# Norm scales spread by transposes of whole tiles, and a convolution whose seven-product jobs keep the program's order on TensorE

## The chip, the cores and the metric

The kernel runs on one core of a Trainium2 chip. The metric is the device time of one execution in microseconds (us); less is better. Before the change the median of three runs is 1405.58 us (1405.56 to 1406.27). The profile comes from one more execution, which took 1405.36 us.

## The reference

The program is one inference step of a decoder with two layers. It works on 512 new prompt tokens and on 8 short sequences of 4 tokens each (32 sample tokens), with the same weights, 1024 channels and all numbers in float32. The first layer mixes by a short gated convolution, the second by retention, and each is followed by a gated feed-forward block. Cut to what matters here:

```
def rmsnorm(x, g):
    y = x * rsqrt(mean(x * x, axis=-1) + 1e-6)
    return y * g

def short_conv_mixer(x, buf, w_in, w_conv, w_out):
    b, c, h = split(x @ w_in, 3)
    full = concatenate([buf, c * h], axis=1)
    y = sum(w_conv[j] * full[:, j:j + L] for j in range(3))
    return (b * y) @ w_out

x = x + mixer(rmsnorm(x));  x = x + swiglu(rmsnorm(x))      # per layer
return rmsnorm(x), states
```

The outputs are the normalised activations and the new states of the convolution and of the retention.

## The kernel before, in words

**Layout.** Activations are kept transposed: eight tiles `x[0..7]` of 128 channels by 544 tokens (512 prompt tokens and 32 sample tokens), each treated as two halves of 272 columns (`HT`). A float32 product is made out of three TensorE products of a faster format: each operand is split into a high and a low part (`split`, L201 to L204: ScalarE rounds, VectorE subtracts), and high by high, high by low and low by high are added in PSUM. Weights come from memory by loads on SyncE's queue and are split in the same way. In `mixed` (L312 to L318) one half of a weight's low part comes from VectorE, and the other from ScalarE (a negated copy) and an adding transfer that GpSimd issues.

**The norm.** `rms_scale` sums the squares of each token over the channels by products with a column (L272), takes the power -0.5 on GpSimd, and has then one scale per token, with 128 tokens down the partitions in one column of `rN`. The scales are needed along the free axis, the same in all 128 partitions. `spread` (L250 to L254) does this with a float32 TensorE product: the column, repeated 128 times, is the stationary operand, and columns `lo:hi` of an identity are streamed. Six spreads cover 544 tokens, because the third tile of tokens lies across the two halves; some are 16, 32 and 112 columns wide. ScalarE copies the result to `R` (L284). `rms_scale` runs four times (convolution, first feed-forward block, retention, second feed-forward block). The final norm calls `spread` in its own function `scale`, three times for each half (L933 to L935).

**Seven-product jobs.** Most of the big matrix products are made by a scheme that multiplies two-by-two blocks with seven block products instead of eight. A `Job` (L364 to L420) makes 256 output channels out of 1024 input channels. It has weights for seven products, which `prepare` makes (`weights7`, L320 to L360: two loads, four VectorE sums, four splits). Each product is 4 channel blocks by 3 parts, so 12 matmuls of 272 columns (`product`, L380 to L393). The results accumulate in three PSUM tiles: `a` takes products 1, 6, 7 and 4 one after the other, `c` takes 5 and 3, and `b` takes 2. After most of them ScalarE or VectorE has to read the tile (`take`, in `summed`, L437 to L450) before the next product adds to it: the first three reads are ScalarE copies (L445), the later ones VectorE additions (L447). `begin` makes product 1, `middle` makes 6, 5, 2 (in an order that can be set; 2, 5, 6 in the convolution's first job) and 7, and `end` makes 3 and 4.

**The order of the work.** `run` (L422 to L435) interleaves the jobs: prepare the next job's weights, the middle of this job, the beginning of the next, the end of this one. In the program's order TensorE's products of two neighbouring jobs n and n+1 are therefore: n's 6, 5, 2, 7; 1 of n+1; n's 3, 4; 6, 5, 2, 7 of n+1; and so on. That isn't yet the order on the chip. The library in which the kernel is written plans each engine's queue while the program is built: among the instructions that it holds to be ready it takes those that stand earlier in the program, and where the earlier ones wait by its reckoning it lets later ones pass. Once planned, a queue's order is fixed. `with tc.issue_after(i):` sets a bound to this planning: what is traced inside the block is queued behind instruction `i` on `i`'s engine. It adds no wait on the chip.

**The convolution.** The first pair of channel tiles, and one third of the second pair, are made by plain products (`project`, L187). Then come eight jobs (L644): two for the rest of the second pair and three for each of the other two pairs. The third job of a pair ends with gating (`mixed_in`, L576 to L582), the second with the convolution's taps (`taps`, L557 to L574), which is a chain of ScalarE and VectorE work. Here the jobs are numbered J0 to J7, and J1:4 is the product 4 of J1. In the trace the product can be told by its operands: `sm<-parts,wh` is 1 or 2, `mm<-parts,h` is 3, `sm<-oh,wh` is 7 or 4, `sm<-oh,h` is 6 and `mm<-oh,h` is 5 (with `ol` or `wl`, `l` in the second and third part). (`oh`, `ol` and `parts` are activations; `wh`, `wl`, `h` and `l` are weights.) The output projection and its loads follow, and then the feed-forward block, whose jobs are of the same class.

Of the kernel before, what the change touches and what calls it, by code (L numbers as in the profile page):

```python
# [12 lines left out]
P = 128  # L13
D = 1024
KT = D // P
SEQ = 512
NB = 8
DS = 4
NS = NB * DS
# [4 lines left out]
HT = T // 2  # L24
# [28 lines left out]
def hybrid_decode_kernel(ctx: ExitStack, tc: tile.TileContext, a: dict, o: dict):  # L53
    nc = tc.nc
# [12 lines left out]
    kinds, at = ["m"], [0]  # L67

    def wide(kind):

        kinds[0], at[0] = kind, 0

    def psum():

        kind = kinds[0][at[0] % len(kinds[0])]
        at[0] += 1
        if kind == "s":
            return [bank(), bank()]
# [21 lines left out]
    mask_s, ident, mean_w = rest[:, :NS], rest[:, NS : NS + P], rest[:, NS + P :]  # L100
# [33 lines left out]
    rN = resid.tile([P, 6], F32, tag="rN", name="rN")  # L134
# [112 lines left out]
            nc.vector.tensor_add(out, var, eps)  # L247
        nc.gpsimd.tensor_tensor(out, out, expo[: out.shape[0], :n], op=ALU.pow)

    def spread(out, tt, lo, hi):  # L250

        return nc.tensor.matmul(
            out, rN[:, tt : tt + 1].to_broadcast([P, P]), ident[:, lo:hi], start=True, stop=True, skip_group_check=True
        )  # L254

    def rms_scale(sample=False, pt=None, rest=4):

        n = 6 if sample else 5  # L260
        pt = pt or psum()
        ms = half(pt, 0)[:, 496:502]
        cols = [slice(tt * P, (tt + 1) * P) for tt in range(4)] + [slice(T - P, T), slice(SEQ, T)]
        for tt in range(n):
            lhs = sqacc[:, cols[tt]]
            if tt == 5:
                lhs = sqlast[:, :P]
                nc.vector.tensor_copy(
                    lhs.rearrange("p (g c) -> p g c", c=NS),
                    sqacc[:, SEQ:].unsqueeze(1).to_broadcast([P, P // NS, NS]),  # L270
                )
            nc.tensor.matmul(ms[:, tt : tt + 1], lhs, mean_w[:, 0:1], start=True, stop=True)  # L272
            if tt < n - 1:
                yield
        rsqrt(rN[:, :n], ms[:, :n], n)
        for _ in range(rest):
            yield

        for tt, hf, at, lo, hi in (
            (0, 0, 0, 0, P), (1, 0, P, 0, P), (2, 0, 2 * P, 0, HT - 2 * P),  # L280
            (2, 1, 0, HT - 2 * P, P), (3, 1, 3 * P - HT, 0, P), (4, 1, SEQ - HT, P - NS, P),
        ):
            spread(half(pt, hf)[:, at : at + hi - lo], tt, lo, hi)
        each(lambda p, r: nc.scalar.activation(r, p, AF.Copy), pt, R)  # L284

    def drain(steps):
# [77 lines left out]
    class Job:  # L364
# [8 lines left out]

        order = (6, 5, 2)
        weave = iter(())

        def prepare(self, adding=False):
            self.w = weights7(*self.srcs, self.sw, len(self.ks) * P, adding, **self.places)

        def product(self, out, which, first):  # L380
            wh, wl = self.w[which]
            for j, k in enumerate(self.ks):
                c = slice(j * P, (j + 1) * P)
                bh, bl = self.operand(k, which)
                for i, (w, b) in enumerate(((wh, bh), (wh, bl), (wl, bh))):
                    last = nc.tensor.matmul(  # L386
                        out, w[:, c], b,
                        start=(first and j == 0 and i == 0), stop=(j == len(self.ks) - 1 and i == 2),
                        skip_group_check=True,
                    )  # L390
                if which not in (5, 6, 2):
                    with tc.issue_after(last.ins):
                        next(self.weave, None)  # L393
# [60 lines left out]
    with ExitStack() as c0:  # L454
# [134 lines left out]
        c, b = temp("c"), temp("b")  # L589
# [52 lines left out]
        turn = [0]  # L642
        pair[1] = c2
        jobs = [job(f, j) for f in range(2, KT, 2) for j in (1, 2, 0) if f > 2 or j != 1]  # L644
        wide("m")
        jobs[0].prepare()
        with ExitStack() as order:
# [14 lines left out]
        for i, n in enumerate(PAIRED[0]):  # L662
            if i < 2:
                wh, wl, pt = early[i]
                project(pt, wh, wl, 0, yh, yl, first=False, ks=(KT - 2, KT - 1))
            else:
                wh, wl = load_piece(a["cvout"][n], KT * P)
                pt = psum()
# [219 lines left out]
    def final(ms, acts, group_weights, fp, tp):  # L888

        ah, al = acts  # L890
        ws = [group_weights(n, ms) for n in range(KT - LATE, KT)]

        sums = {}

        def products(hf):
            c = slice(hf * HT, (hf + 1) * HT)
            for n in range(KT - LATE, KT):
                wh, wl = ws[n - KT + LATE]
                pt = [None, None]
                pt[hf] = bank()  # L900
                project(pt, wh, wl, 0, ah, al, hfs=(hf,))
                nc.vector.tensor_add(x[n][:, c], x[n][:, c], half(pt, hf)[:, :HT])
                square_sum(n, tp, "gu", 4, c=c, add=nc.vector, join=not hf)
                yield

        def gained(hf):

            c = slice(hf * HT, (hf + 1) * HT)
            y = [fp.tile([P, 4, HT], F32, tag="f", name=nm("ya")), tp.tile([P, 4, HT], F32, tag="gu", name=nm("yb"))]
            for kt in range(KT):  # L910
                with tc.issue_after(last_square[0].ins) if hf and kt == KT - 2 else ExitStack():
                    nc.scalar.activation(y[kt // 4][:, kt % 4, :], x[kt][:, c], AF.Copy, scale=g_fin(kt))
            return y

        def scale(hf):
            pt = bank()
            mq = pt[:, 496:499]

            of = (sqacc, sqlast)[: hf + 1]
            for t in of:  # L920
                for i, at in enumerate((0, P, HT - P)):
                    cols = slice(hf * HT + at, hf * HT + at + P)
                    last_sum[hf] = nc.tensor.matmul(
                        mq[:, i : i + 1], t[:, cols], mean_w[:, 0:1], start=t is of[0] and (hf == 0 or i == 0),
                        stop=t is of[-1], skip_group_check=True,
                    )
                if t is not of[-1]:
                    yield
            with tc.issue_after(first_product[0].ins) if hf else ExitStack():
                nc.vector.tensor_scalar_add(rN[:, :3], mq, EPS)  # L930
            powers[hf] = nc.gpsimd.tensor_tensor(rN[:, :3], rN[:, :3], expo[:, :3], op=ALU.pow)
            yield
            for i, (lo, hi) in enumerate(((0, P), (0, P), (3 * P - HT, P))):  # L933
                last_spread[0] = spread(pt[:, i * P : i * P + hi - lo], i, lo, hi)
            sums[hf] = pt[:, :HT]  # L935

        def copied(hf):

            with tc.issue_after(last_square[0].ins):
                nc.scalar.activation(R[:, hf, :], sums[hf], AF.Copy)  # L940

        def out(hf, y, w):

            yy = y[w // 2][:, w % 2 * 2 : w % 2 * 2 + 2, :]
            if w == 0:
                for i in range(2):
                    nc.gpsimd.tensor_tensor(yy[:, i, :], yy[:, i, :], R[:, hf, :], op=ALU.mult)
            else:
                made = nc.vector.tensor_mul(yy, yy, sums[hf].unsqueeze(1).to_broadcast([P, 2, HT]))
                first_product[0] = first_product[0] or made  # L950
# [12 lines left out]
        drain(products(0))  # L963
        first, second = scale(0), products(1)
        next(second)
        next(first)
        y0 = gained(0)
        drain(second)
        drain(first)
        out(0, y0, 1)  # L970
        with tc.issue_after(first_product[0].ins):
            copied(0)
        rest = scale(1)
        with tc.issue_after(last_spread[0].ins):
            next(rest)
        next(rest)
        idle(5, last_sum[1].ins)
        y1 = gained(1)
        out(0, y0, 2)
        out(0, y0, 3)  # L980

        with tc.issue_after(last_store[0].ins), tc.issue_after(powers[1].ins):
            out(0, y0, 0)
        drain(rest)
        copied(1)
        for w in range(4):
            out(1, y1, w)
# [782 lines left out]
```

## Time and profile before

| what | value |
|---|---|
| median of three runs | 1405.58 us (1405.56 to 1406.27) |
| the profiled execution | 1405.36 us |
| its span, first to last instruction | 1403.6 us |
| the plain products of the convolution | about 1 to 58 us |
| the convolution's eight jobs | 58 to 146 us |
| output projection, first feed-forward block | 146 to about 550 us |
| retention | about 550 to 1027 us |
| last output products, second feed-forward block, final norm | 1027 us to the end |

In the profile's rows PE is TensorE's matmuls, PEld its weight loads, DVE VectorE, ACT ScalarE, POOL GpSimd, SP SyncE; "DMA_DIRECT2D" on POOL or SP is the issue of a transfer. A row of the timeline gives the start in us, the duration in us, engine, line, operation, output and inputs, shapes, and how many instructions were merged. Idle time before a row and what ended it stand in brackets. A matmul's row is longer than the step to the next one, since matmuls overlap; the step is read from the starts.

### The profile page before, as it was taken

How to read it: one execution, taken by the hardware profiler on the slowest of the kernel's cores; microseconds unless marked ns; L12 is line 12 of the kernel's file. 1: busy time of each engine (PE TensorE's matmuls, PEld its weight loads, DVE VectorE, ACT ScalarE, POOL GpSimd, SP SyncE). 2: the span in 40 equal slices, each digit the busy share in tenths (PEclk: the TensorE clock that was granted, in tenths of full speed). 3: DMA queues.
4: the chain of work that ended last, by engine and by line, in shares of the span. 5: the costliest groups of instructions: out<-in, count | busy, mean ns of one | idle time of the engine just before them, and what ended most of it. 6: DMA issues, size and time to landing. Idle time of an engine off the chain costs nothing.

```text
span 1403.6 us, 26578 instructions
## 1 busy us (share of the span) xinstructions
PE 1390.2 (99%) x10454; PEld 1317.3 (94%) x10454; DVE 1132.1 (81%) x1923; ACT 822.9 (59%) x1286; POOL 219.4 (16%) x255
## 2 busy tenths in 40 slices
PE   9999999999999999999999999999999999999997
PEld 8999999999999999999967877877899999999997
DVE  6987889898989878676867576586799898989884
ACT  7666567667677657666632313224387767677654
POOL 0111011212221213111200000000111212121212
PEclk9999999999999999999999999999999999999999
DMA  6476346777676754677667355465766777777742
GB/s 206 119 169 166 108 106 159 168 173 183 143 188 151 168 120 134 185 199 201 212 212 240 121 209 184 144 235 181 211 143 153 169 176 172 154 184 153 165 106 87
DMA packets 99295, 233.69 MB, mean 166 GB/s; under 512 B 9793, under 2 KB 33489, under 8 KB 98785
## 3 DMA queue, kind: packets, MB, share of 16 engines
q1 hardware_dynamic: 68032, 167.47, 38.4%
q0 software_dynamic: 28688, 56.61, 23.5%
q10 hardware_dynamic: 2448, 7.91, 1.5%
q8 instruction: 82, 1.34, 0.4%
q14 instruction: 45, 0.36, 0.1%
HBM read 191.84 MB, written 28.42 MB: 157 GB/s over the span
## 4 chain that ended last, share of the span: by engine, by line
PE 93%; DVE 2%; issue 2%; DMA 2%; POOL 0%; ACT 0%; SPq 0%; DVEq 0%; POOLq 0%; ACTq 0%
PE sm L386 43%; PE mm L386 16%; PE mm L187 14%; PE sm L187 4%; PE sm L1262 2%; PE sm L1264 2%; PE sm L1263 2%; PE sm L175 2%; PE sm L177 1%; PE sm L176 1%; PE sm L1483 1%; DVE S L1506 1%; PE mm L1270 1%; DMA wl<-in_rtout_dram 1%; PE mm L1422 0%
## 5 line engine op out<-in xcount | busy, mean ns | idle before, releaser
L386 PE MATMUL sm<-oh,wh 128*128 128x272 f32 x856 | 247.8, 289 | 0.5 <-DVE b L447 0.5
L386 PE MATMUL sm<-ol,wh 128*128 128x272 f32 x856 | 246.1, 288 | 0.0
L386 PE MATMUL sm<-oh,wl 128*128 128x272 f32 x856 | 246.1, 287 | 0.0
L202 ACT ACTIVATE h<-w 128x1024 fp32r<-128x1024 f32 (+3 forms) x170 | 136.5, 804 | 106.3 <-PE mm L386 92.9
L203 DVE TENSOR_TENSOR l<-w,h 128x1024 fp32r<-128x1024 f32 (+3 forms) x170 | 153.6, 904 | 28.1 <-ACT h L202 25.3
L315 ACT ACTIVATE wh<-w 128x1024 fp32r<-128x1024 f32 (+1 forms) x134 | 133.7, 998 | 56.7 <-PE sm L386 48.5
L386 PEld LDWEIGHTS sm<-oh,wh 128*128 128x128 f32 x856 | 161.3, 188 | 2.0 <-DVE b L447 0.9
L386 PEld LDWEIGHTS sm<-oh,wl 128*128 128x128 f32 x856 | 161.1, 188 | 0.0
L386 PEld LDWEIGHTS sm<-ol,wh 128*128 128x128 f32 x856 | 160.8, 188 | 0.1
L386 PE MATMUL sm<-parts,wh 128*128 128x272 f32 x736 | 142.5, 288 | 0.0
L202 ACT ACTIVATE wh<-w 128x1024 fp32r<-128x1024 f32 (+3 forms) x76 | 68.0, 898 | 120.3 <-PE mm L187 62.1
L318 POOL DMA_DIRECT2D wl<-in_ffgu_dram x87 | 81.7, 939 | 328.2 <-ACT wl L317 94.2
L386 PE MATMUL mm<-oh,h 128*128 128x272 f32 x396 | 115.5, 292 | 0.0
L386 PEld LDWEIGHTS sm<-parts,wh 128*128 128x128 f32 x736 | 115.5, 188 | 0.0
L386 PE MATMUL mm<-oh,l 128*128 128x272 f32 x396 | 113.5, 287 | 0.0
L386 PE MATMUL mm<-ol,h 128*128 128x272 f32 x396 | 113.3, 286 | 0.0
L316 DVE TENSOR_TENSOR wl<-w,wh 128x512 fp32r<-128x512 f32 (+1 forms) x134 | 87.2, 651 | 26.4 <-ACT wh L315 26.2
L386 PE MATMUL sm<-parts,wl 128*128 128x272 f32 x368 | 106.2, 289 | 0.3 <-DMA wl<-in_rtqk_dram 0.2
L317 ACT ACTIVATE wl<-wh 128x512 fp32r<-128x512 f32 (+1 forms) x173 | 102.8, 594 | 2.0
L203 DVE TENSOR_TENSOR wl<-w,wh 128x1024 fp32r<-128x1024 f32 (+3 forms) x76 | 79.8, 1055 | 13.1 <-ACT wh L202 12.4
L187 PE MATMUL mm<-parts,wh 128*128 128x272 f32 x488 | 82.4, 290 | 1.4 <-ACT wh L202 1.4
L386 PE MATMUL sm<-oh,h 128*128 128x272 f32 x284 | 82.2, 289 | 0.0
(377 smaller groups left out, 3837.7 us busy)
## 6 DMA issues: line engine op xcount, KB each, us to landing
w<-in_ffgu_dram SPq DMA_DIRECT2D x66, 512.0 KB
wl<-in_ffgu_dram POOLq DMA_DIRECT2D x87, 256.0 KB, 5.2
S<-in_rets_dram SPq DMA_DIRECT2D x16, 1024.0 KB
out_rets_dram<-S SPq DMA_DIRECT2D x16, 1024.0 KB
w<-in_ffdn_dram SPq DMA_DIRECT2D x36, 384.0 KB
cb<-in_ffgu_dram SPq DMA_DIRECT2D x22, 512.0 KB
w<-in_cvin_dram SPq DMA_DIRECT2D x21, 512.0 KB
wl<-in_ffdn_dram POOLq DMA_DIRECT2D x48, 192.0 KB, 4.8
```

What stands on the lines that cost most here:

```text
L175: nc.tensor.matmul(out, lh, rh, start=start, stop=False, skip_group_check=True)
L187: last_product[0] = nc.tensor.matmul(half(pt, hf)[:, :HT], w[:, c], act[k][:, hf * HT : (hf + 1) * HT], start=(first and k == ks[0] and i ...
L202: h = nc.scalar.activation(dh, src, AF.Copy)
L203: last_low[0] = nc.vector.tensor_sub(dl, src, dh.bitcast(F32))
L315: nc.scalar.activation(wh, w, AF.Copy)
L316: last_mixed[0] = nc.vector.tensor_sub(wl[:, :n], w[:, :n], wh[:, :n].bitcast(F32))
L317: nc.scalar.activation(wl[:, n:], wh[:, n:].bitcast(F32), AF.Copy, scale=-1.0)
L318: nc.gpsimd.dma_start(wl[:, n:], src[:, 1, :] if len(src.shape) == 3 else src[:, n:], accum_op=ALU.add)
L386: last = nc.tensor.matmul(out, w[:, c], b, start=(first and j == 0 and i == 0), stop=(j == len(self.ks) - 1 and i == 2), skip_group_check= ...
L1262: nc.tensor.matmul(out, xh[kt][:, ts_], wh[:, cw], start=(kt == 0), stop=False)
L1263: nc.tensor.matmul(out, xh[kt][:, ts_], wl[:, cw], start=False, stop=False)
L1264: last = nc.tensor.matmul(out, xl[kt][:, ts_], wh[:, cw], start=False, stop=(kt == KT - 1))
```

## The change

`spread` becomes a transpose wherever it covers a tile from its first token on, and always covers up to the tile's 128th token. The widths 16 and 32 become 128: the third tile's spread in the first half writes past the 272 columns that are read, and the last one starts at column 144 of the second half and writes tokens again which the one before it has written, with the same values. The 112-column piece stays a product. The jobs of the convolution from the second on are marked `chained`. Each matmul of a marked job is then planned behind the last matmul that any job traced before it. J0's own matmuls aren't bound.

```
-    def spread(out, tt, lo, hi):
+    def spread(out, tt, lo=0):
-        return nc.tensor.matmul(
-            out, rN[:, tt : tt + 1].to_broadcast([P, P]), ident[:, lo:hi], start=True, stop=True, skip_group_check=True
-        )
+        column = rN[:, tt : tt + 1].to_broadcast([P, P])
+        if lo == 0:
+            return nc.tensor.transpose(out, column, ident)
+        return nc.tensor.matmul(out, column, ident[:, lo:], start=True, stop=True, skip_group_check=True)
...
-        for tt, hf, at, lo, hi in (
-            (0, 0, 0, 0, P), (1, 0, P, 0, P), (2, 0, 2 * P, 0, HT - 2 * P),
-            (2, 1, 0, HT - 2 * P, P), (3, 1, 3 * P - HT, 0, P), (4, 1, SEQ - HT, P - NS, P),
+        for tt, hf, at, lo in (
+            (0, 0, 0, 0), (1, 0, P, 0), (2, 0, 2 * P, 0), (2, 1, 0, HT - 2 * P), (3, 1, 3 * P - HT, 0), (4, 1, HT - P, 0),
         ):
-            spread(half(pt, hf)[:, at : at + hi - lo], tt, lo, hi)
+            spread(half(pt, hf)[:, at : at + P - lo], tt, lo)
...
         order = (6, 5, 2)
         weave = iter(())
+        chained = False
+        before = [None]
...
-                    last = nc.tensor.matmul(
-                        out, w[:, c], b,
-                        ...
-                    )
+                    with tc.issue_after(self.before[0].ins) if self.chained and self.before[0] else ExitStack():
+                        last = nc.tensor.matmul(
+                            out, w[:, c], b,
+                            ...
+                        )
+                    self.before[0] = last
...
         jobs = [job(f, j) for f in range(2, KT, 2) for j in (1, 2, 0) if f > 2 or j != 1]
+        for one_job in jobs[1:]:
+            one_job.chained = True
...
-            for i, (lo, hi) in enumerate(((0, P), (0, P), (3 * P - HT, P))):
-                last_spread[0] = spread(pt[:, i * P : i * P + hi - lo], i, lo, hi)
+            for i, at in enumerate((0, P, HT - P)):
+                last_spread[0] = spread(pt[:, at : at + P], i)
```

The last hunk belongs to the final norm.

More of the change, by code (lines that the diff above doesn't have):

```diff
@@ L385, in product @@
                 for i, (w, b) in enumerate(((wh, bh), (wh, bl), (wl, bh))):
-                    last = nc.tensor.matmul(
-                        out, w[:, c], b,
-                        start=(first and j == 0 and i == 0), stop=(j == len(self.ks) - 1 and i == 2),
-                        skip_group_check=True,
-                    )
+                    with tc.issue_after(self.before[0].ins) if self.chained and self.before[0] else ExitStack():
+                        last = nc.tensor.matmul(
+                            out, w[:, c], b,
+                            start=(first and j == 0 and i == 0), stop=(j == len(self.ks) - 1 and i == 2),
+                            skip_group_check=True,
+                        )
+                    self.before[0] = last
                 if which not in (5, 6, 2):
```

## The prediction

> **What bounds the kernel now.** I read the page first, then the busy time by stage, then the chain of waits and the timelines of the convolution.
>
> ```profile
> span 1403.6 us, 26578 instructions
> PE 1390.2 (99%) x10454; PEld 1317.3 (94%) x10454; DVE 1132.1 (81%) x1923; ACT 822.9 (59%) x1286; POOL 219.4 (16%) x255
> PE 93%; DVE 2%; issue 2%; DMA 2%; POOL 0%; ACT 0%; SPq 0%; DVEq 0%; POOLq 0%; ACTq 0%
> ```
>
> TensorE is busy for 99% of the span and has 93% of the chain that ends last. So what shortens TensorE's queue shortens the kernel, and a pause put into that queue lengthens it, unless the pause takes the place of one that is there.
>
> ```profile
> 64.00:68.00 4.00, 4.00 (x33) 3.87 (x32) 2.71 (x5) 4.00 (x8) 1.53 (x2) 1.00 0.69 176
> 68.00:109.00 41.00, 41.00 (x329) 40.87 (x327) 35.31 (x57) 27.69 (x48) 7.13 (x9) 1.00 0.73 173
> 109.00:115.00 6.00, 5.40 (x41) 4.97 (x40) 6.00 (x12) 2.83 (x7) 0.87 (x1) 1.00 0.56 144
> 115.00:146.00 31.00, 30.97 (x247) 30.75 (x246) 24.64 (x38) 18.53 (x31) 4.90 (x6) 1.00 0.64 160
> ```
>
> These are stretches of the job stage: us, length, then busy time and instructions of PE, PEld, DVE, ACT and POOL, the clock, the DMA share and GB/s. TensorE lacks 0.60 us between 109 and 115 us and 0.03 us in the other rows. So ordering its products can win back well under 1 us here. What it can lose depends on whether the present order hides waits.
>
> **The spreads.** One spread of the old kind leaves two records, and one transpose leaves one.
>
> ```profile
> 34.04:35.30 1.26, 1.26 (x12) 1.26 (x12) 1.00 0.03 7
> 1049.24:1050.50 1.26, 1.26 (x12) 1.26 (x12) 1.00 1.03 297
> 1394.38:1395.22 0.84, 0.84 (x6) 0.74 (x6) 1.00 0.11 36
> 705.11 1.06 PE L1321 MATMUL mm<-cb,rot 128*128 128x128 f32 x8
> 705.93 0.47 PE L1263 MATMUL sm<-wl,parts 128*128 128x512 f32 x1
> ```
>
> The first three rows are stretches for the spreads' line alone: six spreads of a norm are 12 records in 1.26 us (first row the convolution's norm, second the second feed-forward block's), so 0.105 us for each record, narrow ones too. The last two rows are eight transposes of 128 by 128 float32, from 705.11 to 705.93 us: 0.103 us each. After the change a norm has five transposes and one product of two records, so 7 records for 12. That saves 5 x 0.105 = 0.53 us on each of four norms, 2.1 us in all. The final norm has 3 records for 6 in each half. Its second half (third row) stands in the tail, where ScalarE's copy and the last VectorE products wait for it: 3 x 0.105 = 0.3 us. Its first half I count at nothing, because the sums of the second half that follow on TensorE wait for squares; without that cover it is 0.3 us more. Sum: **-2.4 us**. The bounds are -2.7 us with that half, and 0, if what comes after each norm waits for something else. I stay near the first, since TensorE is busy in the stages round all four norms.
>
> The Trainium skill, "TensorE: Matmul & The Clock Gate", section "Terms", says that the transpose mode is four times as fast for FP32. By that rule a transpose would take a quarter of a two-record spread, and the spreads would save about 1 us more, an estimate by that page. The eight transposes above say half and not a quarter.
>
> **The order, first place: J0 and J1.** Between them the present order isn't the program's. The chain of waits shows TensorE's products merged by PSUM tile.
>
> ```profile
> 58.15 3.01 PE sm L386 x24
> 61.16 1.49 PE mm L386 x12
> 62.64 4.24 PE sm L386 x33
> 66.88 0.26 PE mm L386 x2
> 67.13 0.37 PE sm L386 x3
> 67.50 0.51 PE mm L386 x3
> 68.02 1.50 PE sm L386 x12
> ```
>
> 24 matmuls take 3.01 us, so one takes 0.125 us. J0 makes products 1 and 2 (24), 5 (12) and 6 (the first 12 of the 33). In the program's order J0:7 is next. But J1:1, J1:2 (the other 21 and 3) and two matmuls of J1:5 pass it, 26 in all, and J0:7 comes at 68.02 us in this view. Why it waits is on ScalarE:
>
> ```profile
> 62.51 1.12 ACT L209 ACTIVATE yh<-b 128x1088 fp32r<-128x1088 f32 x1 [2.24 <-DVE b L579]
> 63.53 1.04 ACT L315 ACTIVATE wh<-w 128x1024 fp32r<-128x1024 f32 x1
> 64.48 1.09 ACT L210 ACTIVATE yl<-yh 128x1088 fp32r<-128x1088 f32 x1
> 65.48 1.04 ACT L202 ACTIVATE h<-w 128x1024 fp32r<-128x1024 f32 x1
> 66.43 0.62 ACT L317 ACTIVATE wl<-wh 128x512 fp32r<-128x512 f32 x1
> 66.95 0.38 ACT L445 ACTIVATE h<-mm 128x272 f32<-128x272 f32 x1
> 67.22 0.39 ACT L445 ACTIVATE h<-sm 128x272 f32<-128x272 f32 x1
> ```
>
> J0:7 adds to the tile of J0:6, and that tile must first be copied (last row, done at 67.61 us). J0:3 adds to the tile of J0:5, which the row before copies (done at 67.33 us). J0:6 had ended near 64.0 us. Ahead of both copies stand the gating's split and the split of J1's weights, which come earlier in the program, so the planner has no reason to move them. With the change J1:1 is bound behind J0:7, and nothing else is ready: J0:3 and J0:4 need the same copies, and the output projection needs products that don't exist yet. TensorE stands from about 64.0 to 67.3 us, and the 26 matmuls come afterwards: 26 x 0.125 = **+3.25 us**. The rest of the stretch costs nothing more: J1's copies and J2's split of weights, which needs a weight buffer freed by J1:2 or J0:4, move back by about as much as the products that need them. The bounds are 0, if the planner gives ScalarE the copies first, and 3.4 us, the whole wait. If only the first copy goes ahead of L209, which was ready within a few tenths of it, J0:3 fills 12 x 0.125 = 1.5 us, and 1.75 us stay. I take 3.25 us, which is nearest to the rows.
>
> **The order, second place: J4 and J5.**
>
> ```profile
> 111.43 0.29 PE L386 MATMUL sm<-oh,h 128*128 128x272 f32 x1
> ...
> 113.69 0.28 PE L386 MATMUL mm<-oh,h 128*128 128x272 f32 x1
> 114.43 0.40 PE L386 MATMUL sm<-oh,wh 128*128 128x272 f32 x1 [0.46 <-DVE b L447]
> ```
>
> From 111.43 to 113.69 us there are 19 matmuls, J5:6 (12) and seven of J5:5. The program has J4:4 first, and that starts at 114.43 us, after VectorE's addition of J4:7.
>
> ```profile
> 94.91 6.33 DMA w<-in_cvin_dram
> ...
> 101.33 0.69 DVE w L337
> ...
> 113.68 0.71 DVE b L447 x2
> 114.43 1.77 PE sm L386 x12
> ```
>
> The chain of waits says what makes it late: a load of weights that lands at 101.24 us, then VectorE's sums for the weights, the taps, and only then the addition. The load began when a weight buffer came free behind products of J2, so it moves with TensorE's shift of 3 us, and the wait stays. In the program's order the 19 matmuls come after J4:4 instead of before it: 19 x 0.125 = **+2.4 us** on top of the wait that is there. The bounds are 0, when the shift lets VectorE catch up, and 3.0 us (111.43 to 114.43). I take 2.4 us. What is queued behind the waiting product is all of TensorE; VectorE and ScalarE wait for it in turn, and afterwards the rows from 115 to 146 us have no idle time that could give it back.
>
> A third crossing costs nothing.
>
> ```profile
> 80.38 0.39 PE L386 MATMUL sm<-oh,wh 128*128 128x272 f32 x1
> 82.00 0.29 PE L386 MATMUL sm<-oh,l 128*128 128x272 f32 x1
> 79.90 0.43 DVE L447 TENSOR_TENSOR b<-b,sm 128x272 f32<-128x272 f32 x1
> ```
>
> J1:4 starts here in the middle of J2:6, after an addition that ends at 80.33 us. Shifted by 3 us, J1:4 is due near 82.5 us, and its addition is late by less than that, since J0:4 before it shifts by only half. Chained or not, the jobs of the feed-forward blocks aren't touched.
>
> The Trainium skill, "TensorE: Matmul & The Clock Gate", section "The mechanism", says that matmuls keep strict first-in, first-out order. It speaks against this change, and the pause at 113.69 us agrees; if waiting products could be passed on the chip, both places would cost nothing.
>
> **The sum.** -2.4 + 3.25 + 2.4 = +3.25 us on the profiled execution's 1405.36 us gives 1408.6. The median shown is 0.2 us higher than that execution. Forecast: **1408.7 us**, slower by 0.22%.
>
> **The rivals.** (1) Only one of the two places costs. Then it is 1405.36 - 2.4 + 3.25 = 1406.2 or 1405.36 - 2.4 + 2.4 = 1405.4. For it speaks that the second place hangs on a load that may land early, and the first on ScalarE's order within tenths; against it that each wait is seen in the rows. (2) On the other side, no longer slower: the planner, which sees the late product, puts ScalarE's copies ahead of the splits. The place is 62.5 to 67.6 us, and it decides if J0:6's copy comes before L210, so by 64.5 us. Then J0:7 starts near 65 us, the shift is small, the load at 94.91 us starts sooner, and only the spreads are left: 1405.36 - 2.4 = 1403.0; with the 0.6 us that TensorE lacks from 109 to 115 us it is 1402.4. Against it: copies already wait behind splits that come earlier in the program. (3) The shifted buffers make a third pause of about 2 us, the size of the other two: 1410.7. For it speaks that weight buffers are freed by products and that loads then start later; against it that from 115 us on the order is already the program's and TensorE doesn't wait. (4) The transposes don't do what is said: with a repeated column as operand they leave two records each and save nothing, 1411.0; or they go four times as fast, 1407.6 with both pauses.
>
> **How the numbers follow.** Chances: forecast 0.40, (1) 0.22, (2) 0.22, (3) 0.12, (4) 0.04. A measurement of this kernel can tell about 0.2% from no change, so the bounds lie at 1402.8 and 1408.4. The forecast's own range is 1407.2 to 1409.8, and some 0.27 of its 0.40 lies above 1408.4; with (3) and a part of (4), slower has 0.40. Of (2) half lies under 1402.8, which with a little luck elsewhere makes faster 0.12. The same has 0.48. The range 1402.6 to 1410.8 leaves out about 2 in 10.
>
> **What would show it.** Right: TensorE idle for about 3 us before J0:7 near 64 us, with ScalarE's copy as the releaser; J4:4 ahead of J5:6, with 3 us idle and VectorE's addition as the releaser; 7 records in about 0.74 us at each norm. Wrong: no idle time at either place, or ScalarE's copies ahead of L210; a transpose step over 0.2 us; or a change in the feed-forward or retention stages as large as these.

## The result

The kernel after takes 1413.71 us (median of six runs, 1410.27 to 1415.1), the kernel before on the same chip 1405.67 us (six runs, 1405.05 to 1406.27). The ratio is 1.0055, with a 95% interval of 1.0042 to 1.0068, so the change makes the kernel slower by about half a per cent. The forecast was 1408.7 us, and the result lies above the top of its range, 1410.8. The profiled execution took 1410.27 us, the fastest of the six. The kernel's lines have moved by a few: L386 is now L389, L445 is L449, L447 is L451, and the spreads are L254 (transposes) and L255 (the product that stays).

From the page of the kernel after, the span, the engines, and the chain that ended last:

```profile
span 1408.5 us, 26527 instructions
PE 1388.1 (99%) x10428; PEld 1315.0 (93%) x10428; DVE 1133.3 (80%) x1923; ACT 823.5 (58%) x1286; POOL 219.8 (16%) x255
PE 90%; DVE 5%; DMA 2%; ACT 2%; issue 1%; POOL 0%; DVEq 0%; SPq 0%; POOLq 0%; ACTq 0%
```

TensorE has 2.1 us less to do (1388.1 after 1390.2), and the span is still 4.9 us longer. VectorE has taken 3 points of the chain. So the lost time is waiting. The waits of TensorE in the kernel after (engine and line, who ended the wait, us in total, times, longest):

```profile
PE sm L389 <- DVE b L451: 4.7, 2, 2.4
PE sm L389 <- ACT h L449: 2.7, 1, 2.7
...
PE mm L389 <- ACT c L449: 0.5, 2, 0.3
```

In the kernel before the convolution's jobs had one wait, 0.5 us, at 114.43 us, which the prediction shows. Now there are three long ones. The busy time by stage of the kernel after gives their places (columns as in the prediction):

```profile
63.90:66.70 2.80, 0.16 (x2) 0.00 (x0) 1.55 (x3) 2.79 (x5) 1.38 (x2) 1.00 1.01 268
66.80:80.20 13.40, 13.40 (x107) 13.40 (x108) 10.30 (x17) 7.51 (x15) 1.97 (x3) 1.00 0.64 141
80.40:82.80 2.40, 0.14 (x2) 0.00 (x0) 2.40 (x6) 0.63 (x1) 0.00 (x0) 1.00 0.81 176
...
115.10:117.50 2.40, 0.14 (x2) 0.00 (x0) 2.40 (x6) 0.63 (x1) 0.00 (x0) 1.00 0.84 184
```

TensorE stands before J0:7, before J1:4 and before J4:4, and is full between the first and the second. In the first pause ScalarE is busy for all 2.8 us, in the other two VectorE is. The timeline of TensorE in the kernel after gives the lengths, here those of the second and the third:

```profile
80.25 0.28 PE L389 MATMUL mm<-parts,l 128*128 128x272 f32 x1
82.88 0.39 PE L389 MATMUL sm<-oh,wh 128*128 128x272 f32 x1 [2.34 <-DVE b L451]
...
114.96 0.28 PE L389 MATMUL mm<-parts,l 128*128 128x272 f32 x1
117.60 0.40 PE L389 MATMUL sm<-oh,wh 128*128 128x272 f32 x1 [2.35 <-DVE b L451]
```

From start to start these are 2.63 and 2.64 us, where a step is 0.125. Read in the same way, the pause before J0:7 is 2.97 us (63.77 to 66.75), and two small ones before J2:3 and J5:3 are 0.56 us each. So the losses are 2.84 + 2.50 + 2.51 + 2 x 0.43 = 8.7 us, where TensorE lacked 0.6 us in the kernel before.

The spreads did what they were to do. TensorE's timeline of the kernel after at the convolution's norm, three transposes, the product with its two records, two transposes, then the next product:

```profile
33.02 0.49 PE L254 MATMUL mm<-cb,rN 128*128 128x128 f32 x3
33.35 0.37 PE L255 MATMUL mm<-cb,rN 128*128 128x112 f32 x2
33.56 0.38 PE L254 MATMUL mm<-cb,rN 128*128 128x128 f32 x2
33.70 0.74 PE L187 MATMUL mm<-parts,wh 128*128 128x272 f32 x4
```

Seven records take 0.7 us, where twelve took 1.26, and a transpose takes 0.11 us, where the product of two records takes 0.21. So a transpose is twice as fast here. The Trainium skill, "TensorE: Matmul & The Clock Gate", section "Terms", has the rule that the prediction weighed, four times as fast; these rows don't show that, and the measurement decides.

All the signs that the prediction named for being right are there: TensorE idle before J0:7 with ScalarE's copy as the releaser, J4:4 ahead of J5:6 after a wait for VectorE's addition (2.7 and 2.35 us idle, where about 3 were said), and seven records in 0.7 us at the norm. They test the terms that the sum had, not those that it left out.

### The profile page after: what moved, and what is told of

Read it like the earlier page. It is cut to its first block, busy times and chain, and to the rows that moved or that the text cites. A ratio compares the mean times of both kernels' runs of the same rounds, so it can differ in the third digit from the quotient of the medians.

```text
span 1408.5 us, 26527 instructions
## 1 busy us (share of the span) xinstructions
PE 1388.1 (99%) x10428; PEld 1315.0 (93%) x10428; DVE 1133.3 (80%) x1923; ACT 823.5 (58%) x1286; POOL 219.8 (16%) x255
## 4 chain that ended last, share of the span: by engine, by line
PE 90%; DVE 5%; DMA 2%; ACT 2%; issue 1%; POOL 0%; DVEq 0%; SPq 0%; POOLq 0%; ACTq 0%
PE sm L389 42%; PE mm L389 16%; PE mm L187 13%; PE sm L187 4%; PE sm L1268 2%; PE sm L1270 2%; PE sm L1269 2%; PE sm L175 1%; PE sm L177 1%; PE sm L176 1%; PE sm L1489 1%; DVE S L1512 1%; PE mm L1276 1%; DMA rot<-km 1%; PE mm L1428 0%
## 5 line engine op out<-in xcount | busy, mean ns | idle before, releaser
L389 PE MATMUL sm<-oh,wh 128*128 128x272 f32 x856 | 248.0, 290 | 7.4 <-DVE b L451 4.7
L389 PE MATMUL sm<-ol,wh 128*128 128x272 f32 x856 | 246.1, 288 | 0.0
L389 PE MATMUL sm<-oh,wl 128*128 128x272 f32 x856 | 246.0, 287 | 0.0
L389 PEld LDWEIGHTS sm<-oh,wh 128*128 128x128 f32 x856 | 161.3, 188 | 9.3 <-DVE b L451 5.4
L389 PEld LDWEIGHTS sm<-oh,wl 128*128 128x128 f32 x856 | 161.0, 188 | 0.0
L389 PEld LDWEIGHTS sm<-ol,wh 128*128 128x128 f32 x856 | 160.8, 188 | 0.1
L389 PE MATMUL sm<-parts,wh 128*128 128x272 f32 x736 | 142.4, 288 | 0.0
L389 PE MATMUL mm<-oh,h 128*128 128x272 f32 x396 | 115.5, 292 | 0.0
L389 PEld LDWEIGHTS sm<-parts,wh 128*128 128x128 f32 x736 | 115.4, 188 | 0.0
L389 PE MATMUL mm<-oh,l 128*128 128x272 f32 x396 | 113.4, 286 | 0.0
L389 PE MATMUL mm<-ol,h 128*128 128x272 f32 x396 | 113.2, 286 | 0.0
L389 PE MATMUL sm<-parts,wl 128*128 128x272 f32 x368 | 106.1, 288 | 0.3 <-DMA wl<-in_rtqk_dram 0.2
L389 PE MATMUL sm<-oh,h 128*128 128x272 f32 x284 | 82.3, 290 | 0.4 <-ACT g L449 0.3
```

The lines of the kernel that those rows point to most:

```text
L389: last = nc.tensor.matmul(out, w[:, c], b, start=(first and j == 0 and i == 0), stop=(j == len(self.ks) - 1 and i == 2), skip_group_check= ...
```

## The experiments

Each group of four ran on one chip, beside the kernel before, which took 1404.84, 1404.96 and 1405.17 us there (medians). Each ratio is to that. "Clock" is the mean granted TensorE clock of an execution; it is 0.998 or 0.999 in every execution of the kernel before. In the tables "pause" is the length from the start of the last matmul to the start of the next.

### The parts apart

The first four runs are the kernel after again, its transposes alone, its bound jobs alone, and its transposes with only the last three jobs bound.

```
e0_again: the kernel after
e1_transposes: the kernel after without
-        for one_job in jobs[1:]:
-            one_job.chained = True
e2_chain: the kernel before, and only the bound jobs added
e3_chain_from_j5: the kernel after with
-        for one_job in jobs[1:]:
+        for one_job in jobs[5:]:
```

> The changed kernel once more, unaltered. Theory: TensorE's three pauses of about 2.9, 2.5 and 2.5 us before J0:7, J1:4 and J4:4 (and two of 0.5 us before J2:3 and J5:3) are fixed in the queue, so they show again at the same places; the spread of the times (1410.3 to 1415.1) comes from the granted clock, which falls after a pause in some executions. Expected 1410 to 1415 us, and in a profile of 1412 us or more a stretch of half clock of some us right behind a pause. Rival: the spread has nothing to do with the pauses (transfers, say); then the clock by stage is 1.00 in a slow profile too, and the lost time lies in other stages.

> Transposes alone: no job is chained. Theory: TensorE's order in the convolution is that of before, no pause over 0.8 us, and 7 records for 12 at each norm: 1405.6 - 2.4 = 1403.2 us (1402.5 to 1404.0), clock as before. Rival: the transposes themselves move the planner's order or lower the clock (they are the only new operation); then it is at 1408 us or more with a mean clock under 0.998.

> The order alone: the old spreads, the jobs chained from the second on. Theory: all of the loss is here. The three long pauses and two short ones, 9.0 us where the kernel before has 1.8 us, give 1405.6 + 7 = 1412.6 us, and up to 1417 us when the clock falls after a pause. Rival (the loss needs the transposes): within 2 us of 1405.6.

> Transposes, and the order bound only from the sixth job (J5) on. Theory: the pauses before J0:7 and J1:4 go, that before J4:4 (2.5 us) and the short one before J5:3 (0.5 us) stay; against transposes alone that is +3.0 less the 1.0 us that TensorE waits there anyway: 1405.2 us, up to 1408.5 if one such pause is enough for the clock to fall. Rival (the pauses hang together, J4:4's being the echo of J0:7's): no pause at J4:4, 1403.2 us.

| run | median us | ratio, 95% interval | pauses of TensorE in the job stage |
|---|---|---|---|
| e0_again | 1411.55 | 1.0044 (1.003 to 1.0058) | 2.97 before J0:7, 2.64 before J1:4, 2.64 before J4:4 |
| e1_transposes | 1408.25 | 1.0023 (1.0014 to 1.0032) | 3.38 in J2:2 |
| e2_chain | 1415.89 | 1.0075 (1.0061 to 1.0088) | 3.51 before J0:3 and J0:7, 2.63 before J1:4, 2.64 before J4:4 |
| e3_chain_from_j5 | 1410.79 | 1.004 (1.0027 to 1.0053) | 3.19 in J2:2, 2.58 before J4:4 |

The bound jobs alone bring all three pauses, and e2's time is within what was expected. It is 4.3 us above e0's: the spreads, some 2.7 us, and the first pause, 0.5 us, are longer, and the clock of its four executions is 0.995 to 0.996, where e0's is 0.996 to 0.998. In e3 the pause before J4:4 comes without the two others, so it isn't their echo; its time misses the 1405.2 us that was expected because of a pause that the transposes bring. e0's profile fell on an execution of 0.998, so the stretch of half clock that was expected in a slow one couldn't show there. The surprise is e1: with no job bound the transposes alone make the kernel slower, where 2.4 us less was expected. The timeline of TensorE of e1_transposes:

```profile
73.01 0.41 PE L389 MATMUL sm<-parts,wh 128*128 128x272 f32 x2
...
74.77 0.41 PE L389 MATMUL sm<-parts,wh 128*128 128x272 f32 x2
78.27 0.60 PE L389 MATMUL sm<-parts,wl 128*128 128x272 f32 x1 [3.10 <-DMA wl<-in_cvin_dram]
```

From 73.01 us on J2:1 runs, then two matmuls of J2:5, and from 74.77 us the first of J2:2, all ahead of J1:7, J1:3 and J1:4. The kernel before has J2:1 at 76.2 us and J2:2 at 84. The planner has pulled them ahead in its plan, and on the chip the low part of J2:2's weights is still on its way: it comes by an adding transfer from memory, and TensorE stands for 3.1 us behind it, with J1's products 7, 3 and 4 queued behind. So the transposes cost nothing as operations; they move a plan. The planned queues bear this out: of the instructions in the convolution 20 on VectorE and 18 on ScalarE stand elsewhere than in the kernel before. That is as many as when only the first, the second or the fifth of the six spreads is made a transpose, with the same queues on all engines but for the spreads themselves; with the sixth alone nothing else moves, with the third alone hardly anything. (These are the queues of built programs; none with a single transpose ran.) Why the planner's reckoning tips over there no run shows.

The clock is the second surprise. The busy time by stage of e1_transposes, from the end of its pause:

```profile
78.27:81.48 3.21, 3.21 (x14) 3.21 (x15) 1.82 (x3) 0.31 (x2) 0.00 (x0) 0.50 0.83 160
81.60:84.60 3.00, 3.00 (x26) 3.00 (x26) 0.58 (x2) 0.18 (x2) 0.00 (x0) 1.00 0.22 85
```

PEclk, the third number from the right, is 0.50 in the first row: for 3.41 us (78.07 to 81.48) TensorE has half its clock, and 14 matmuls take 3.21 us, where 26 take 3.00 in the second row. That is up to 1.7 us more, on top of the pause. In e2_chain the same comes after the pause before J1:4, not after the longer one at 63 us:

```profile
64.00:66.90 2.90, 0.16 (x1) 0.16 (x2) 1.65 (x3) 2.90 (x5) 1.06 (x2) 1.00 0.86 234
81.90:84.30 2.40, 0.16 (x2) 0.00 (x0) 2.40 (x6) 0.63 (x1) 0.00 (x0) 1.00 0.89 189
85.67:89.08 3.41, 3.41 (x18) 3.41 (x17) 3.25 (x5) 1.86 (x3) 0.64 (x1) 0.50 0.07 19
```

### Undoing the suspected causes

```
f1_bind_product2: transposes everywhere; in the jobs from J2 on, product 2 alone is bound,
behind the last product of the job before (its product 4)
-  with tc.issue_after(self.before[0].ins) if self.chained and self.before[0] else ExitStack():
+  with tc.issue_after(self.before[0].ins) if self.chained and which == 2 else ExitStack():
f2_old_spread_in_conv: no job bound; transposes but for the convolution's norm
+  if rest == 5:
+      ... spread_old(half(pt, hf)[:, at : at + hi - lo], tt, lo, hi)
f3_filled: the kernel after, and behind J0:3, J1:3 and J4:3
+  for _ in range(self.fill):
+      with tc.issue_after(self.before[0].ins):
+          self.before[0] = nc.tensor.matmul(other[0][:, :P], ones, ones, start=True, stop=True)
...
+  jobs[0].fill, jobs[1].fill, jobs[4].fill = 12, 10, 10
f4_late_prepare: the kernel after, and in run, for the convolution's first job
+  if late and i == 0:
+      job.middle()
       nxt.prepare()
+  else:
       ...    (prepare, then middle, as in the kernel after)
```

> Edit: transposes everywhere; of the jobs, only product 2 of the jobs from the third on is bound, behind the last product of the job before it. Theory A (with transposes alone the loss is the planner's: it pulls J2:2 ahead, whose low weights are still in flight, and TensorE stands 3.38 us at 74.9 us): that pause is gone, the granted clock has no half-rate window behind it, and the time is that of the transposes alone without the pause and without the window: 1408.25 - 3.4 - 1.4 = 1403.5 us, ratio to the kernel before 0.9985 to 0.9995. Rival B (the order is disturbed in more than one place, and the next product that was pulled ahead takes over the wait): a pause of 2 to 3 us stays between 72 and 97 us, time 1406 to 1408, ratio 1.001 to 1.002. Rival C (the transposes themselves cost more than the products they replace): no pause, yet ratio over 1.001.

> Edit: the old spreads in the convolution's norm alone, transposes in the other three norms and in the final norm, no job bound. Theory A (the transposes save TensorE's records, and what they cost comes only through the planner's order in the convolution): three norms at 0.53 us and 0.3 us in the final norm are saved, no new pause in the convolution: 1.9 us less than the kernel before on the same chip, ratio 0.9987 (0.9980 to 0.9995), 7 records in 0.74 us at each of the three norms. Rival B (the saving is hidden, since ScalarE's copies or the products behind each norm wait for something else): ratio 0.9995 to 1.0005 with the records gone. Rival C (transposes lower the clock or pass slowly): ratio over 1.0005, and bursts of the spreads over 1 us or a granted clock below that of before.

> Edit: the kernel after, with matmuls of ones put into TensorE's queue where it pauses: 12 behind J0:3, 10 behind J1:3, 10 behind J4:3; they write to a half of a tile that nobody reads. Theory A (the kernel after is 1410.3 to 1415.1 us because some of its executions lose clock after a pause of 2.6 to 3.0 us, and the loss needs an idle TensorE): waits stay as long as they are, but TensorE isn't idle in them, so no half-rate window follows; times close together near the lowest of after, 1409.5 to 1411, clock 0.998 in every execution. Rival B (the spread of the times has nothing to do with idle time): times spread over 4 us as those of after, clock 0.995 to 0.998. Rival C (filling matmuls delay the products behind the waits): over 1412.

> Edit: the kernel after, with the first job's copies ahead of the second job's loads and splits in the program, so that ScalarE has the copies first. Theory A (J0:7 waits 2.97 us because ScalarE's copies stand behind splits of J1's weights and of the gating): the pause before J0:7 falls below 1 us, perhaps with a wait of up to 1 us before J1:1, whose weights are split later; time 2 us less than after, near 1409, ratio to the kernel before 1.002 to 1.004. Rival B (the splits are needed as soon as the copies, so the pause only moves to J1:1 or J1:2): 2.5 to 3.5 us of pause between 62 and 70 us all the same, ratio 1.004 to 1.007.

| run | median us | ratio, 95% interval | pauses | clock |
|---|---|---|---|---|
| f1_bind_product2 | 1405.41 | 1.0002 (0.9993 to 1.0011) | none over 0.91 | 0.998 to 0.999 |
| f2_old_spread_in_conv | 1403.51 | 0.9987 (0.9978 to 0.9995) | none over 0.76 | 0.998 to 0.999 |
| f3_filled | 1411.6 | 1.0044 (1.0031 to 1.0056) | filled | 0.998 to 0.999 |
| f4_late_prepare | 1409.95 | 1.0032 (1.002 to 1.0043) | 2.58 before J1:4, 2.64 before J4:4 | 0.996 to 0.998 |

**f2** is the clean test of the spreads. With the old spreads in the convolution's norm the planned queues of ScalarE, VectorE, GpSimd and SyncE are those of the kernel before, and TensorE's differs by the spreads alone. It is faster than both kernels. Against the kernel before that is 0.13%, about 1.8 us (interval 0.05 to 0.22%; the medians lie 1.45 us apart), and three norms and the final norm were to bring 1.9 us. Its only wait of TensorE between 60 and 120 us is the old one:

```profile
PE sm L402 <- DVE b L464: 0.5, 1, 0.5
```

**f1** takes away the pause in J2:2 and the half clock after it, as theory A said, and lands between the two theories in time. Its waits between 60 and 120 us say why in part: in place of one late product there are four.

```profile
PE mm L391 <- DVE l L203: 0.6, 1, 0.6
PE sm L391 <- DVE b L454: 0.5, 1, 0.5
PE mm L391 <- ACT b L452: 0.4, 1, 0.4
PE sm L391 <- DVE c L454: 0.4, 1, 0.4
```

That is 1.9 us where f2 has 0.5. With the 0.5 us that its convolution's norm saves this explains 0.9 of the 1.9 us between f1 and f2; the other 1.0 us isn't accounted for.

**f4** puts ScalarE's copies ahead of the splits (and J0's middle ahead of J1's loads). Its timeline of ScalarE, where L453 are the copies for J0:3 and J0:7:

```profile
62.18 0.38 ACT L453 ACTIVATE h<-mm 128x272 f32<-128x272 f32 x1
62.46 1.11 ACT L210 ACTIVATE yl<-yh 128x1088 fp32r<-128x1088 f32 x1
63.47 0.39 ACT L453 ACTIVATE h<-sm 128x272 f32<-128x272 f32 x1
63.74 1.06 ACT L202 ACTIVATE h<-w 128x1024 fp32r<-128x1024 f32 x1
```

The pause before J0:7 is gone, so ScalarE's order made it. The other two stay, and in this profile the one before J1:4 costs clock as well (busy time by stage of f4_late_prepare):

```profile
62.50:67.00 4.50, 4.50 (x37) 4.43 (x36) 3.21 (x6) 3.88 (x6) 1.16 (x2) 1.00 0.55 145
77.70:80.20 2.50, 0.23 (x2) 0.01 (x1) 2.50 (x6) 0.63 (x1) 0.00 (x0) 1.00 0.78 143
80.79:84.20 3.41, 3.41 (x17) 3.41 (x16) 2.66 (x5) 1.51 (x3) 0.00 (x0) 0.50 0.21 80
```

**f3** gives TensorE other matmuls to do while the products wait. In these stretches (of f3_filled) it isn't idle:

```profile
62.00:68.00 6.00, 5.99 (x50) 5.80 (x49) 4.57 (x9) 4.47 (x7) 1.72 (x2) 1.00 0.71 185
80.00:84.00 4.00, 3.90 (x33) 3.71 (x32) 4.00 (x9) 0.63 (x1) 0.00 (x0) 1.00 0.74 194
114.00:119.00 5.00, 4.88 (x41) 4.68 (x41) 5.00 (x11) 0.87 (x2) 0.36 (x1) 1.00 0.63 157
```

All five executions keep a clock of 0.998 or more; of the ten executions of the kernel after with its pauses (with e0) seven have 0.995 to 0.997. So the lost clock needs an idle TensorE. But the time is that of e0 (ratio 1.0044 both): 1409.35 to 1412.51 us, a spread of 3.2 us without any loss of clock. In its profile the fill ends with the wait (J0:7 starts 0.06 us after its copy), so a delay by the fill doesn't explain that. That part of theory A missed: the runs spread by 3 us for other reasons too, as those of the kernel before do.

### One job bound at a time

These four start from f2, so the spreads play no part in the convolution, and bind J1, J2, both, or J5.

```
g_j1        +  jobs[1].chained = True
g_j2        +  jobs[2].chained = True
g_j1_j2     +  jobs[1].chained = jobs[2].chained = True
g_j5        +  jobs[5].chained = True
```

> Edit: old spread in the convolution's norm, transposes elsewhere (the kernel of the run with ratio 0.9987), and of the jobs J1 alone bound, each of its products behind the one before it. Theory A (each bound job costs where its predecessor's late product stands, and VectorE's order is planned anew): a pause of 3.0 to 3.5 us before J0:7, none before J1:4, where J2:6 and a part of J2:5, 19 matmuls or 2.4 us, go ahead of it while VectorE's addition is late; time 1403.5 + 3.3 = 1406.8, up to 1.7 more where the clock drops after the pause; ratio 1.0005 to 1.0025. Rival B (the first place costs less, since the shift is won back behind it): ratio 0.9985 to 1.0. Rival C (J1's binding brings the pause before J1:4 by itself): two pauses, ratio over 1.0028.

> Edit: the same base, of the jobs J2 alone bound behind J1:4. Theory A (without J1's binding VectorE has the addition for J1:4 where the kernel before has it; only the 8 matmuls of J2:6 that went ahead of J1:4 come behind it): a pause of 1.0 us (8 x 0.125) before J1:4, time 1404.5, ratio 0.9990 to 1.0000. Rival B (binding J2 is what costs 2.5 us there): a pause of 2.5 us, ratio 1.0000 to 1.0012. Rival C, the step of the prediction (the crossing costs nothing): no pause, ratio 0.9985 to 0.9989.

> Edit: the same base, J1 and J2 both bound. Theory A (the two together make the third pause: J1's binding moves the addition on VectorE behind the taps' products with R and a split, J2's binding takes away the 2.4 us of products that covered it): pauses of 3.0 to 3.5 us before J0:7 and of 2.3 to 2.7 us before J1:4, time 1403.5 + 3.3 + 2.5 = 1409.3, up to 1.7 to 3.4 more where the clock drops after them; ratio 1.0025 to 1.0055. Rival B (costs only add: J1's 3.3 and J2's 1.0): ratio 1.0010 to 1.0025.

> Edit: the same base, of the jobs J5 alone bound behind J4:4. Theory A (the second place costs what it covered, 19 matmuls or 2.4 us, also without any shift of the jobs before it): one pause of 2.3 to 3.0 us before J4:4, time 1403.5 + 2.4 = 1405.9, up to 1.7 more where the clock drops; ratio 1.0000 to 1.0015. Rival B (the wait there needs the shift of J0 to J3): no pause, ratio 0.9985 to 0.9992.

| run | median us | ratio, 95% interval | to f2 | pauses | clock |
|---|---|---|---|---|---|
| g_j1 | 1408.09 | 1.002 (1.0011 to 1.0029) | +4.6 | 3.52 before J0:3 and J0:7 | 0.995 to 0.997 |
| g_j2 | 1403.17 | 0.9985 (0.9976 to 0.9994) | -0.3 | 1.16 before J1:4 | 0.998 to 0.999 |
| g_j1_j2 | 1409.61 | 1.0034 (1.0021 to 1.0046) | +6.1 | 3.51 before J0:3 and J0:7, 2.63 before J1:4 | 0.996 to 0.997 |
| g_j5 | 1406.66 | 1.001 (1.0001 to 1.0019) | +3.2 | 3.15 before J4:4 | 0.996 to 0.999 |

The column "to f2" compares medians from two chips, on which the kernel before differs by 0.2 us. The longest waits of TensorE in g_j1, in g_j2, in g_j1_j2 and in g_j5, one fence each:

```profile
PE mm L402 <- ACT h L462: 3.2, 1, 3.2
```

```profile
PE sm L402 <- DVE b L464: 0.9, 1, 0.9
```

```profile
PE mm L402 <- ACT h L462: 3.2, 1, 3.2
PE sm L402 <- DVE b L464: 2.3, 1, 2.3
```

```profile
PE sm L402 <- DVE b L464: 2.9, 1, 2.9
```

Each pause came where theory A put it; g_j5's is a little longer than the 2.3 to 3.0 us that were expected. J1 alone costs its first place and no more before J1:4, because 19 matmuls of J2 go ahead of J1:4 and cover a late addition. J2 alone brings a pause of 1.0 us over a step there, the eight matmuls of J2:6 that no longer go ahead. Both together cost 2.5 us there, which is more than the sum. The reason is in VectorE's queue. First its rows in the kernel before; the addition at 79.90 us, which the prediction quotes, stands between these two:

```profile
77.05 2.93 DVE L563 SCALAR_TENSOR_TENSOR y<-u,vec,y 128x560 f32<-128x560 f32 x4
...
80.25 1.22 DVE L572 TENSOR_TENSOR y<-y,R 128x1024 f32<-128x1024 f32 x1
```

And in the kernel after:

```profile
76.72 2.94 DVE L567 SCALAR_TENSOR_TENSOR y<-u,vec,y 128x560 f32<-128x560 f32 x4
79.57 0.68 DVE L316 TENSOR_TENSOR wl<-w,wh 128x512 fp32r<-128x512 f32 x1
80.17 1.22 DVE L576 TENSOR_TENSOR y<-y,R 128x1024 f32<-128x1024 f32 x1
81.31 0.69 DVE L203 TENSOR_TENSOR l<-cb,h 128x512 fp32r<-128x512 f32 x1
81.91 0.22 DVE L577 TENSOR_TENSOR y<-y,R 128x64 f32<-128x64 f32 x1
82.05 0.78 DVE L451 TENSOR_TENSOR b<-b,sm 128x272 f32<-128x272 f32 x2
```

The taps (L563, now L567) end 0.3 us earlier, but the addition has lost its place right behind them: a split, two products with R, another split and J1's addition of product 2 (the first of the two in the last row) stand first, about 2.8 us of work. VectorE has no idle time between, and no late load holds it. Its rows have the addition in this place in all of e2, f4, g_j1 and g_j1_j2, which bind J1, and in its old place in f2 and g_j2. At J4:4 it stands like that in the kernel before already:

```profile
111.12 0.69 DVE L316 TENSOR_TENSOR wl<-w,wh 128x512 fp32r<-128x512 f32 x1
...
113.60 0.78 DVE L447 TENSOR_TENSOR b<-b,sm 128x272 f32<-128x272 f32 x2
```

With J1 bound the crossing of J1:4 is planned like that of J4:4: late addition, 19 matmuls ahead to cover it. J2's binding then takes the cover away. In g_j2 the pause shows in the trace and not in the time, whose ratio is the one of rival C. There the 0.5 us wait before J4:4 is gone, which gives back half of it; the rest is below what the runs tell apart.

## Why the prediction was wrong

**The step that failed** is "A third crossing costs nothing". It cost 2.50 us, nearly as much as each of the other two, and with it the prediction's sum is 1411.1. Rival (3) has nearly that time (1410.7), but by another mechanism: it expected loads that start late, and here VectorE's order is what changed. The prediction took VectorE's order as given and only shifted it: the addition was to be late "by less than that". But binding TensorE's queue made the planner plan VectorE's anew, and the addition went 2.8 us down the queue. g_j2 has the addition in its old place and loses 1.0 us at J1:4 in its trace, g_j1_j2 has it in the new one and loses 2.5 us. Had the prediction read VectorE's rows at both places, it would have seen the addition right behind the taps at the one and behind five more operations at the other, and so how little holds it in its place. Even with the old order "nothing" was wrong: the row at 80.38 us shows J1:4 in the middle of J2:6, and the eight matmuls before it were as much a cover as the 19 before J4:4.

**What wasn't seen at all** is the clock. The five slower executions of the kernel after have a mean clock of 0.995 to 0.997, the profiled one 0.998. A half-clock stretch of 3.41 us is 0.0012 of the span's clock and costs up to 1.7 us. In the ten executions of the kernel after and of e0 the time goes with the clock: 1410.1 to 1410.92 us at 0.998, 1412.17 and 1412.6 at 0.997, 1413.52 to 1415.1 at 0.996 and 0.995. One or two stretches on top of the profiled 1410.27 us give up to 1412.0 or 1413.7, so most of the rest is clock, and up to 1.4 us stay open, within the 3 us by which f3 and the kernel before spread without such loss. For the five this is inferred, since no trace of them exists; such stretches are shown in the traces of e1, e2, f4, g_j1, g_j1_j2 and g_j5.

The ledger, for the profiled execution:

| term | predicted us | measured us |
|---|---|---|
| spreads | -2.4 | -2.7 in the trace (f2, without the convolution's: about -1.8 in time) |
| J0:7 behind ScalarE's copy | +3.25 | +2.84 (g_j1, alone: +3.39) |
| J4:4 behind VectorE's addition | +2.4 | +1.9 (2.51, less the 0.6 that was there) |
| J1:4 behind VectorE's addition | 0 | +2.50 |
| J2:3 and J5:3 behind ScalarE's copies | 0 | +0.9 |
| sum | +3.25 | +5.4 |

The spreads' -2.7 us is counted from the first spread to the next matmul: 1.26, 1.36, 1.26 and 1.26 us at the four norms before, 0.68, 0.73, 0.68 and 0.68 after, and 0.31 us less in the tail. 1405.36 + 5.4 is 1410.8, and the execution took 1410.27. Its first spreads start at 33.02 us instead of 34.04, so 1.0 us of gain lies ahead of all that was changed (a wait of 1.16 us for ScalarE near 8.7 us doesn't come in it); 0.5 us the other way isn't accounted for.

**The spreads** were right in size, and f2 shows a gain of that size in the time itself. What the prediction didn't ask is what the shorter norm does to the plan. In e1 that loses 3.4 us of pause and up to 1.7 us of clock, and the kernel is slower without a single bound job.

**The first place** was right in mechanism and nearly in size. g_j1, where ScalarE has its old order, stands from 63.92 to 67.44 us, where the prediction said 64.0 to 67.3. In the kernel after the planner does put one copy ahead, as the prediction had it for its smaller value of 1.75 us:

```profile
61.08 0.40 ACT L449 ACTIVATE h<-mm 128x272 f32<-128x272 f32 x1 [2.12 <-PE mm L389]
61.38 1.11 ACT L209 ACTIVATE yh<-b 128x1088 fp32r<-128x1088 f32 x1
...
65.79 0.62 ACT L202 ACTIVATE h<-w 128x512 fp32r<-128x512 f32 x1
66.31 0.38 ACT L449 ACTIVATE h<-sm 128x272 f32<-128x272 f32 x1
```

J0:3 then does fill 1.5 us. But the copy for J0:7 has one more split ahead of it (65.79 us), while TensorE came there 1.6 us earlier, so most of what J0:3 gained is lost.

**The second place** was right: 2.51 us from the matmul before, against 2.4 and the wait that was there. g_j5 shows that it needs no shift of the jobs before. The wait ends with VectorE's addition in both, as forecast.

Rival (1) falls, since both places cost; so does rival (4), since transposes leave one record of 0.11 us. Rival (2), the planner puts the copies first, came true for one copy of two; f4 shows that both are worth 2.9 us of pause.

## What to carry to other kernels

An order bound on one engine makes the planner plan the other queues again; here VectorE's and ScalarE's moved. So look up, for each product that no longer lets others pass, which instruction it waits for and what stands ahead of that instruction on its own engine; a product that crossed another was covering something, and the cover has to be priced at every crossing. Before a small gain is tied to a riskier edit, measure it by itself with the other queues unchanged: here about 1.8 us were there to have (f2, 0.9987), in three norms of four and the final norm. An edit that is cheaper as an operation can still cost more than it saves where it tips a plan, so compare the planned queues and not only the instruction counts.

## What the runs showed of the hardware

A pause of TensorE costs more than its length when it falls badly. In each trace the granted clock goes from half to full once near the start (7.01 us in the kernel after, 5.69 in f4). If stretches of 3.41 us are counted from that moment, every half-clock stretch in the job stage begins and ends on such a boundary: in f4 80.79 is 5.69 + 22 x 3.413. All 18 pauses of over 2.5 us in the profiles, each cut by these boundaries, give this:

| longest part of a pause inside one stretch | pauses | followed by half clock |
|---|---|---|
| 1.34 to 1.97 us | 12 | 0 |
| 2.14 to 3.24 us | 6 | 6 |

So in e2 the 3.51 us pause at 63 us, cut into 1.97 and 1.54, costs no clock, and the 2.63 us pause at 82 us, cut into 0.49 and 2.14, does. The limit lies between 1.97 and 2.14 us here (from 1.81 to 2.14 if a pause is counted from the end of the last matmul instead of its start), and since the phase changes from execution to execution, so does the time: g_j5 has 1404.9 to 1406.95 us at a clock of 0.998 or 0.999 and 1406.66 to 1408.3 at 0.996 or 0.997. The Trainium skill, "TensorE: Matmul & The Clock Gate", section "What's actually happening", has the window: 3413 ns, running freely. That agrees with 3.41 us. It says that the clock halves after an idle window; here a window idle for 63% was enough, and the measurement decides.
